# Turning the third and part of the fourth chunk of x2 while the second norm is found, in a trunk-layer kernel on one core

## The chip, the cores and the metric

The kernel runs on one core of one Trainium2 chip. The metric is the device time of one execution in microseconds (us); the median of several runs is given. The core's engines are TensorE (PE: matrix products and transposes, its weight loads are shown apart as PEld), VectorE (DVE), ScalarE (ACT), GpSimd (POOL) and SyncE (SP, which issues most DMAs).

## The reference

One transformer layer on 128 context tokens and 256 latent tokens, 384 in all, with model width 2048 and feed-forward width 5632, in float32. The part around the change, cut to what matters:

```python
x = x + g1 * token_mixing(...)                 # ends in a product with w_o
h2 = rms_norm(x, n2) * (1 + sc2) + sh2         # rms_norm(x, g) = x * rsqrt(mean(x*x) + eps) * g
a, g = split(h2 @ w_gate_up, 2)
x = x + g2 * ((silu(g) * a) @ w_down)
```

Context and latent tokens have different sc2, sh2, g1 and g2, so that every operation with them is done for two ranges of tokens.

## The kernel before

**Precision and weight units.** Every matrix product is done as three: both operands are split into a high and a low part (`split`, lines 133 to 135: the high part is a cast on ScalarE, L134, the low part a subtraction on VectorE, L135), and `mm3` (L138 to L140) adds high x high, high x low and low x high. Weights come in units of two blocks of 128 rows by 512 columns. `next_unit` splits the next loaded unit, steps the pieces of side work in `front` and `behind`, and returns the oldest split unit, whose matmuls are issued after it. Tags `wh` and `wl` have three buffers each, so a unit can be split when the third unit before it has been used up on TensorE; the units that are split and not yet used stand in the queue `ready`. In the last unit of the product with w_o nothing is split (`late`), so that ScalarE and VectorE are free for the norm; `split_unit` makes up for it after the first step of `normed`.

**Order.** The schedule is written out: each engine runs its instructions in the order in which the code issues them, and waits for others by semaphores. Side work is a Python generator in a `Paced`, which one tick of `next_unit` steps once.

**PSUM.** Eight banks: four buffers of tag `mm8` (`mm_tile`), three of tag `at8` (`at_tile`) and one for the modulation rows. `acc_tile` takes accumulators from a ring of four mm and then three at buffers. A new tile gets a buffer whose last user is done with it.

**Around the change.** The product with w_o runs over four chunks of 512 columns (`cc`), each with three accumulators (one for each 128 tokens) and eight units. After a chunk's last unit, `x2[cc]` = residual + gate x product (L1125, L1126), and the squares are summed for each token into `ssx[:, t, cc]` (L1128). In the next chunk's loop `transposed(cc - 1)` turns the chunk: for each 128 of its columns (`kt` counts them, 0 to 15), three TensorE transposes into one at buffer (L1096) and two ScalarE evictions with the norm's gain and modulation into `x2T` (L1098). So chunks 0, 1 and 2 are turned in the loops of chunks 1, 2 and 3.

After chunk 3 the norm is found: the reduction of `ssx` (L1132), then `inv_sqrt` (L152 to L159: mean and eps, square root on ScalarE, reciprocal and one Newton step). Its result per token, `r2`, is spread over the partitions by three transposes (L1140) and copied to `rB` (L1142). Then `normed` makes the operand h of the feed-forward part in steps of two `kt`: product with `rB` (L1148, VectorE), high parts with the shift (L1153, ScalarE), low parts (L1159, VectorE). Its first step runs before the feed-forward loop, each further one in a `next_unit`, so the step for the `kt` that a unit needs is issued one unit ahead. The steps k0 = 2, 4, 6, 8 also turn and evict one `kt` each of chunk 3 (12 to 15).

The first half of the feed-forward loop (`half` 1, part 0) has eight units, each 24 matmuls into four accumulators: unit u needs h of kt = u and u + 1. `facc` is None until the last of them, where the buffers for the rest are taken.

Of the kernel before, what the change touches and what calls it, by code (L numbers as in the profile page):

```python
# [13 lines left out]
F32 = mybir.dt.float32  # L14
F32R = mybir.dt.float32r
AF = mybir.ActivationFunctionType
ALU = mybir.AluOpType
AX = mybir.AxisListType

P = 128  # L20
D = 2048
KT = D // P
# [5 lines left out]
CTX = 128  # L28
LAT = 256
TOK = CTX + LAT  # L30
NT = TOK // P
# [64 lines left out]
def trunk_kernel(ctx: ExitStack, tc: tile.TileContext, io: dict):  # L96
    nc = tc.nc
# [26 lines left out]
    small = ctx.enter_context(tc.tile_pool(name="small", bufs=4))  # L124
# [19 lines left out]
        warm = small.tile([P, 1], F32, tag="warm", bufs=1, name=nm("warm"))  # L144
        nc.scalar.activation(out=warm, in_=ones[:, 0:1], func=AF.Sqrt)

    def inv_sqrt(out, ssq, n, shape):

        v = small.tile(shape, F32, tag="rs_v", name=nm("rsv"))
        s = small.tile(shape, F32, tag="rs_s", name=nm("rss"))  # L150
        t = small.tile(shape, F32, tag="rs_t", name=nm("rst"))
        nc.vector.tensor_scalar(v, ssq, 1.0 / n, EPS, op0=ALU.mult, op1=ALU.add)  # L152
        yield
        nc.scalar.activation(out=s, in_=v, func=AF.Sqrt)
        yield
        nc.vector.reciprocal(s, s)
        nc.vector.scalar_tensor_tensor(out=t, in0=s, scalar=-0.5, in1=s, op0=ALU.mult, op1=ALU.mult)
        nc.vector.tensor_mul(t, t, v)
        nc.vector.scalar_tensor_tensor(out=out, in0=t, scalar=1.5, in1=s, op0=ALU.add, op1=ALU.mult)  # L159
# [24 lines left out]
    front, behind = [], []  # L184
# [14 lines left out]
    def next_unit(late=False):  # L199

        for p in front:
            p.tick()
        if not late:
            split_unit()
        for p in front + behind:
            p.tick()
        loads.more()
        return ready.popleft()


    ident = consts.tile([P, P], F32, tag="ident", name="ident")
# [36 lines left out]
    msc = [consts.tile([P, KT, 2], F32, tag=f"msc{i}", name=f"msc{i}") for i in range(2)]  # L248
# [9 lines left out]
    with ExitStack() as ph:  # L258
# [7 lines left out]
        def at_tile():  # L266
            return pa.tile([P, CH], F32, tag="at", name=nm("at"))
# [3 lines left out]
        def acc_tile():  # L271

            return next(ring)()
# [146 lines left out]
        with ExitStack() as pha:  # L420
# [16 lines left out]
            for cc in range(4):  # L437
                t = c6([P, NT, CH], "xc")
# [14 lines left out]
            for j in range(2):  # L453
# [10 lines left out]
                out=csz[:, :, 0:2], in_=pt[:, 0:32].rearrange("p (c k) -> p k c", c=2), func=AF.Silu  # L464
# [5 lines left out]
            ssx = small.tile([P, NT, 4], F32, tag="ssx", bufs=1, name="ssx")  # L470
# [25 lines left out]
            ss1 = small.tile([P, NT], F32, tag="ss1", bufs=1, name="ss1")  # L496
            nc.vector.tensor_reduce(out=ss1, in_=ssx, axis=AX.X, op=ALU.add)
            r1 = small.tile([P, NT], F32, tag="r1", bufs=1, name="r1")
# [112 lines left out]
            for gi, (k0, n) in enumerate(GROUPS):  # L611
# [3 lines left out]
                for ci in ORDER:  # L615
# [3 lines left out]
                    for u in range(k0, k0 + n, 2):  # L619
# [3 lines left out]
                        for t in range(NT):  # L623
                            sl = slice(t * P, (t + 1) * P)
# [455 lines left out]
    def load_residual(cc):  # L1080
# [6 lines left out]
        rows_until(2)  # L1087
        yield from load_rows(xtp, 2, cc)

    def transposed(cc):  # L1090

        for k in range(4):
            kt = cc * 4 + k
            o = at_tile()
            for t in range(NT):
                nc.tensor.transpose(o[:, t * P : (t + 1) * P], x2[cc][:, t, k * P : (k + 1) * P], ident)  # L1096
            for cnd, sl in ((0, slice(0, CTX)), (1, slice(CTX, TOK))):
                nc.scalar.activation(  # L1098
                    out=x2T[cc][:, k, sl], in_=o[:, sl], func=AF.Copy, scale=msc[1][:, kt, cnd : cnd + 1]
                )  # L1100
            yield

    rows.rate = RATES[3]
# [1 line left out]
    for cc in range(4):  # L1105
        xin[cc] = xtp.tile([P, NT, CH], F32, tag="xin", bufs=2, name=nm("xin"))
        behind.append(Paced(load_residual(cc)))
        po = [acc_tile() for _ in range(NT)]
        for u in range(0, KT, 2):
            if cc == 3 and u == KT - 4:  # L1110
                rows.rate = 0
            if cc == 3 and u == 8:
                warm_sqrt()
            wH, wL = next_unit(late=cc == 3 and u == KT - 2)
            if u == 2 and cc:
                rows_until(4)
                behind.append(Paced(transposed(cc - 1)))
            for t in range(NT):
                sl = slice(t * P, (t + 1) * P)
                for kk in range(2):  # L1120
                    k = u + kk
                    mm3(po[t], mixH[k][:, sl], mixL[k][:, sl], wH[:, kk], wL[:, kk], k == 0, k == KT - 1)
                if u == KT - 2:
                    d = tmp.tile([P, CH], F32, tag="d", name=nm("d"))
                    nc.vector.tensor_mul(d, po[t], gb[cc][:, min(t, 1)])  # L1125
                    nc.vector.tensor_add(x2[cc][:, t], xin[cc][:, t], d)  # L1126
                    junk = tmp.tile([P, CH], F32, tag="junk", name=nm("junk"))
                    nc.scalar.activation(  # L1128
                        out=junk, in_=x2[cc][:, t], func=AF.Square, accum_out=ssx[:, t, cc : cc + 1]
                    )  # L1130
    ss2 = small.tile([P, NT], F32, tag="ss1", bufs=1, name="ss2")
    nc.vector.tensor_reduce(out=ss2, in_=ssx, axis=AX.X, op=ALU.add)  # L1132
    r2 = small.tile([P, NT], F32, tag="r1", bufs=1, name="r2")
    for _ in inv_sqrt(r2, ss2, D, [P, NT]):
        pass
    rows_until(3)
    last_chunk = transposed(3)
    o = mm_tile()
    for t in range(NT):
        nc.tensor.transpose(o[:, t * P : (t + 1) * P], r2[:, t : t + 1].to_broadcast([P, P]), ident)  # L1140
    rB = tmp.tile([P, TOK], F32, tag="rB", bufs=1, name="rB")
    nc.scalar.copy(rB, o[:, :TOK])  # L1142

    def normed():
        for k0 in range(0, KT, 2):
            for kt in (k0, k0 + 1):
                v = x2T[kt // 4][:, kt % 4]
                nc.vector.tensor_mul(v, v, rB)  # L1148
            for kt in (k0, k0 + 1):
                H, L = new_h(kt)  # L1150
                v = x2T[kt // 4][:, kt % 4]
                for cnd, sl in ((0, slice(0, CTX)), (1, slice(CTX, TOK))):
                    nc.scalar.activation(  # L1153
                        out=H[:, sl], in_=v[:, sl], func=AF.Identity, bias=msh[1][:, kt, cnd : cnd + 1]
                    )
            for kt in (k0, k0 + 1):
                v = x2T[kt // 4][:, kt % 4]
                for cnd, sl in ((0, slice(0, CTX)), (1, slice(CTX, TOK))):
                    nc.vector.scalar_tensor_tensor(  # L1159
                        out=hL[kt][:, sl], in0=v[:, sl], scalar=msh[1][:, kt, cnd : cnd + 1],  # L1160
                        in1=fr(hH[kt][:, sl]), op0=ALU.add, op1=ALU.subtract,
                    )
            if k0 in (2, 4, 6, 8):
                next(last_chunk)
            yield

    norm = Paced(normed())
# [6 lines left out]
    facc = None  # L1174
# [21 lines left out]
    for part, nf in enumerate(FF_PARTS):  # L1196
# [4 lines left out]
        cL = [None] * nf  # L1201
        for c4 in range(nf // 4):
            for half in (1, 0):
                po = [acc_tile() for _ in range(4)]
                for u in range(0, KT, 2):
                    wH, wL = next_unit()
                    if u == KT - 2 and facc is None:
                        norm.drain()
                        rows.rate = RATES[4]
                        pho.close()  # L1210
                        actp = phf.enter_context(tc.tile_pool(name="actp", bufs=1))
                        facc = [actp.tile([P, NT, CH], F32, tag=f"fa{i}", name=f"facc{i}") for i in range(4)]
                        ftmp = phf.enter_context(tc.tile_pool(name="tmpf", bufs=2))
                    for f in range(4):
                        s = slice(f * P, (f + 1) * P)
                        for kk in range(2):
                            k = u + kk
                            mm3(po[f][:, :TOK], wH[:, kk, s], wL[:, kk, s], hH[k], hL[k], k == 0, k == KT - 1)
                        if u < KT - 2:
                            continue  # L1220
                        if half:
                            if f == 0:
                                sg = ftmp.tile([P, 4, TOK], F32, tag="sg", name=nm("sg"))
                            nc.scalar.activation(out=sg[:, f], in_=po[f][:, :TOK], func=AF.Silu)
                        else:
                            i = c4 * 4 + f
                            nc.vector.tensor_mul(sg[:, f], sg[:, f], po[f][:, :TOK])
                            cH[i] = actp.tile([P, TOK], F32R, tag=f"cH{i}", name=nm("cH"))
                            cL[i] = actp.tile([P, TOK], F32R, tag=f"cL{i}", name=nm("cL"))
                            if nf == 4:  # L1230
                                split(cH[i], cL[i], sg[:, f])
            if nf > 4:
                behind.append(Paced(split_act(c4 * 4, sg, cH, cL), 2))
# [74 lines left out]
```

## Time and profile before

| | us |
|---|---|
| median of 3 runs (lowest, highest) | 2082.51 (2082.15, 2085.05) |
| the profiled execution | 2081.68 |
| its span, first to last instruction | 2079.9 |
| PE busy | 2045.1 (98%) |
| DVE busy | 1210.2 (58%) |
| ACT busy | 755.3 (36%) |
| POOL busy | 57.6 (3%) |
| mean granted TensorE clock | 0.998 of full speed |

The times of the prediction are us from the start of the span. The part that matters lies between the last loop of the product with w_o (its last matmul starts at 958.77) and the end of the first feed-forward half (about 1003.7). A busy TensorE isn't TensorE at its peak: matmuls overlap in the records, so a row's length is more than the distance to the next one's start. In a timeline, what stands in brackets is the idle time of the engine before the row, and what ended it.

### The profile page before, as it was taken

What the parts mean: (1) busy time and instruction counts of PE and PEld (TensorE: products, weight loads), DVE (VectorE), ACT (ScalarE), POOL (GpSimd) and SP (SyncE); (2) the same over time, 40 slices, a digit from 0 to 9 for tenths busy, and PEclk for the clock granted to TensorE, in tenths of its full rate; (3) what the DMA queues carried; (4) which work ended last, traced back from release to release, by engine and by line L of the source; (5) the groups of instructions that cost most, each with busy time, mean ns of one, the idle gap of its engine ahead of it and who ended that gap; (6) DMA issues with size and microseconds to landing.
All of it is one profiled execution on the core that took longest, in us unless ns stands there. A gap on an engine that the chain in (4) does not pass through costs nothing.

```text
span 2079.9 us, 27373 instructions
## 1 busy us (share of the span) xinstructions
PE 2045.1 (98%) x10963; PEld 1846.3 (89%) x10963; DVE 1210.2 (58%) x1418; ACT 755.3 (36%) x1146; POOL 57.6 (3%) x101
## 2 busy tenths in 40 slices
PE   6999999999999999998999999999999999999999
PEld 4668888999999999887998899899989998999897
DVE  4635899687885787665544454444454434333456
ACT  5323232456665443335333332223322232233222
POOL 3000000000001000001000000000000000000000
PEclk9999999999999999999999999999999999999999
DMA  9886878677775775753554555445454444444453
GB/s 343 287 321 212 299 246 306 208 215 226 221 218 156 262 247 174 263 189 116 162 159 145 155 160 155 145 146 157 158 153 140 122 126 128 124 130 122 132 162 121
DMA packets 219999, 390.45 MB, mean 188 GB/s; under 512 B 28080, under 2 KB 64960, under 8 KB 219872
## 3 DMA queue, kind: packets, MB, share of 16 engines
q1 hardware_dynamic: 212704, 382.13, 57.9%
q10 hardware_dynamic: 4672, 6.31, 0.8%
q8 instruction: 86, 1.41, 0.3%
q0 software_dynamic: 2496, 0.27, 0.1%
q14 instruction: 41, 0.34, 0.0%
HBM read 371.81 MB, written 20.51 MB: 189 GB/s over the span
## 4 chain that ended last, share of the span: by engine, by line
PE 93%; DVE 2%; DMA 2%; ACT 1%; issue 1%; SPq 1%; ACTq 0%; DVEq 0%
PE mm L138 19%; PE mm L139 19%; PE mm L140 19%; PE at L138 11%; PE at L139 11%; PE at L140 11%; DMA wm<-in_w_mod 1%; PE md L387 1%; DVE accr L311 1%; PE at L847 1%; PE at L915 1%; DVE wl L135 1%; DMA xc<-in_x_sample 0%; SPq L365 0%; PE md L321 0%
## 5 line engine op out<-in xcount | busy, mean ns | idle before, releaser
L135 DVE TENSOR_TENSOR wl<-wraw,wh 128x1024 fp32r<-128x1024 f32 (+1 forms) x464 | 559.5, 1206 | 711.1 <-ACT wh L134 710.1
L134 ACT CAST wh<-wraw 128x1024 fp32r<-128x1024 f32 (+1 forms) x464 | 480.1, 1036 | 1044.3 <-PE at L139 292.6
L138 PE MATMUL mm<-hH,wh 128*128 128x384 f32 x1216 | 410.7, 338 | 3.9 <-ACT gst L981 2.3
L140 PE MATMUL mm<-hH,wl 128*128 128x384 f32 x1216 | 406.8, 334 | 0.0
L139 PE MATMUL mm<-hL,wh 128*128 128x384 f32 x1216 | 406.4, 334 | 0.0
L311 DVE SCALAR_TENSOR_TENSOR accr<-wmr,csz,accr 128x1024 f32<-128x1024 f32 x240 | 304.8, 1278 | 0.0
L138 PE MATMUL at<-hH,wh 128*128 128x384 f32 x704 | 236.5, 336 | 1.4 <-ACT hH L1153 1.4
L138 PEld LDWEIGHTS mm<-hH,wh 128*128 128x128 f32 x1216 | 228.4, 188 | 9.5 <-ACT gst L981 3.5
L139 PE MATMUL at<-hL,wh 128*128 128x384 f32 x704 | 236.3, 336 | 0.0
L140 PE MATMUL at<-hH,wl 128*128 128x384 f32 x704 | 235.8, 335 | 0.0
L139 PEld LDWEIGHTS mm<-hL,wh 128*128 128x128 f32 x1216 | 228.4, 188 | 0.0
L140 PEld LDWEIGHTS mm<-hH,wl 128*128 128x128 f32 x1216 | 228.2, 188 | 0.0
L138 PE MATMUL mm<-wh,hH 128*128 128x512 f32 x431 | 172.6, 400 | 0.0
L139 PE MATMUL mm<-wl,hH 128*128 128x512 f32 x431 | 168.5, 391 | 1.7 <-DVE wl L135 1.7
L140 PE MATMUL mm<-wh,hL 128*128 128x512 f32 x431 | 168.1, 390 | 0.0
L138 PE MATMUL mm<-wh,cH 128*128 128x512 f32 x352 | 139.3, 396 | 0.0
L139 PE MATMUL mm<-wl,cH 128*128 128x512 f32 x352 | 139.2, 396 | 0.0
L140 PE MATMUL mm<-wh,cL 128*128 128x512 f32 x352 | 139.2, 396 | 0.0
L138 PEld LDWEIGHTS at<-hH,wh 128*128 128x128 f32 x704 | 132.7, 188 | 2.8 <-ACT hH L1153 1.8
L139 PEld LDWEIGHTS at<-hL,wh 128*128 128x128 f32 x704 | 132.7, 188 | 1.1 <-DVE hL L1159 0.7
L140 PEld LDWEIGHTS at<-hH,wl 128*128 128x128 f32 x704 | 132.6, 188 | 0.0
L138 PEld LDWEIGHTS mm<-wh,hH 128*128 128x128 f32 x431 | 81.0, 188 | 30.8 <-issue 9.8
(240 smaller groups left out, 2387.7 us busy)
## 6 DMA issues: line engine op xcount, KB each, us to landing
wraw<-in_w_gate_up SPq DMA_DIRECT2D x176, 512.0 KB, 3.7
wmr<-in_w_mod SPq DMA_DIRECT2D x128, 512.0 KB, 4.2
wraw<-in_w_down SPq DMA_DIRECT2D x88, 512.0 KB, 3.7
wm<-in_w_mod SPq DMA_DIRECT2D x64, 512.0 KB, 6.7
wraw<-in_w_gate SPq DMA_DIRECT2D x64, 512.0 KB, 5.1
wraw<-in_w_in SPq DMA_DIRECT2D x56, 512.0 KB, 5.9
wraw<-in_w_o SPq DMA_DIRECT2D x32, 512.0 KB, 5.2
wraw<-in_w_fnet_proj SPq DMA_DIRECT2D x16, 512.0 KB, 6.0
```

Source lines behind the costliest of these rows:

```text
L134: nc.scalar.copy(H, x)
L135: nc.vector.tensor_sub(L, x, fr(H))
L138: nc.tensor.matmul(out, aH, bH, start=start, stop=False)
L139: nc.tensor.matmul(out, aH, bL, start=False, stop=False)
L140: nc.tensor.matmul(out, aL, bH, start=False, stop=stop)
L311: nc.vector.scalar_tensor_tensor(out=acc[:, cnd], in0=wm, scalar=sc, in1=acc[:, cnd], op0=ALU.mult, op1=ALU.add)
L387: nc.tensor.matmul(pm[q : q + 32, :w], csz[:, k, :], wm[:, ty, kk + par, :], start=k < 2, stop=k >= KT - 2, tile_position=(0, q), skip_gro ...
L847: nc.tensor.matmul(po[j][:, cols], qx[rows[j], q], kx[rows[j], k], start=i == 0, stop=i == 2, tile_position=(j * HD, 0),)
L915: nc.tensor.transpose(o[:, i * P : (i + 1) * P], sc[:, j, c0 : c0 + P], ident)
```

## The change

Chunk 2 (kt 8 to 11) is no longer turned in the loop of chunk 3. Turning is cut in two functions: `turn` issues the transposes and keeps the tile in a queue `held`, `gained` issues the two evictions of the oldest tile there. After the norm, kt 8 and 9 are turned and evicted and kt 10 is turned; then come the transposes of `r2` and the copy to `rB`; then kt 11 and 12 are turned. Each step of `normed` evicts one held tile behind its own work and turns the next kt (13, 14, 15), until none is left. The reduction of `ssx` takes chunks 0 to 2 ahead of the last unit's matmuls, with the first operation of `inv_sqrt`; the sum of chunk 3 is added behind its squares by one operation. The accumulators of the first feed-forward half come from mm buffers alone and not from the ring.

```diff
-    def inv_sqrt(out, ssq, n, shape):
+    def inv_sqrt(out, ssq, n, shape, more=None):
...
         nc.vector.tensor_scalar(v, ssq, 1.0 / n, EPS, op0=ALU.mult, op1=ALU.add)
         yield
+        if more is not None:
+            nc.vector.scalar_tensor_tensor(out=v, in0=more, scalar=1.0 / n, in1=v, op0=ALU.mult, op1=ALU.add)
         nc.scalar.activation(out=s, in_=v, func=AF.Sqrt)
...
+    held = deque()
+
+    def turn(kt):
+        o = at_tile()
+        for t in range(NT):
+            nc.tensor.transpose(o[:, t * P : (t + 1) * P], x2[kt // 4][:, t, kt % 4 * P : (kt % 4 + 1) * P], ident)
+        held.append((kt, o))
+
+    def gained():
+
+        kt, o = held.popleft()
+        for cnd, sl in ((0, slice(0, CTX)), (1, slice(CTX, TOK))):
+            nc.scalar.activation(
+                out=x2T[kt // 4][:, kt % 4, sl], in_=o[:, sl], func=AF.Copy, scale=msc[1][:, kt, cnd : cnd + 1]
+            )
+
     def transposed(cc):
...
+        for kt in range(cc * 4, cc * 4 + 4):
+            turn(kt)
+            gained()
             yield
...
             wH, wL = next_unit(late=cc == 3 and u == KT - 2)
+            if cc == 3 and u == KT - 2:
+                ss2 = small.tile([P, NT], F32, tag="ss1", bufs=1, name="ss2")
+                nc.vector.tensor_reduce(out=ss2, in_=ssx[:, :, 0:3], axis=AX.X, op=ALU.add)
+                r2 = small.tile([P, NT], F32, tag="r1", bufs=1, name="r2")
+                norm = inv_sqrt(r2, ss2, D, [P, NT], ssx[:, :, 3])
+                next(norm)
             if u == 2 and cc:
                 rows_until(4)
-                behind.append(Paced(transposed(cc - 1)))
+                if cc < 3:
+                    behind.append(Paced(transposed(cc - 1)))
...
-    ss2 = small.tile([P, NT], F32, tag="ss1", bufs=1, name="ss2")
-    nc.vector.tensor_reduce(out=ss2, in_=ssx, axis=AX.X, op=ALU.add)
-    r2 = small.tile([P, NT], F32, tag="r1", bufs=1, name="r2")
-    for _ in inv_sqrt(r2, ss2, D, [P, NT]):
+
+    for _ in norm:
         pass
     rows_until(3)
-    last_chunk = transposed(3)
+    late = iter(range(8, KT))
+    for _ in range(2):
+        turn(next(late))
+        gained()
+    turn(next(late))
     o = mm_tile()
...
     nc.scalar.copy(rB, o[:, :TOK])
+    for _ in range(2):
+        turn(next(late))
...
-            if k0 in (2, 4, 6, 8):
-                next(last_chunk)
+            if held:
+                gained()
+            for kt in late:
+                turn(kt)
+                break
             yield
...
-                po = [acc_tile() for _ in range(4)]
+                po = [(acc_tile if facc else mm_tile)() for _ in range(4)]
```

More of the change, by code (lines that the diff above doesn't have):

```diff
@@ L1088, in load_residual @@
         yield from load_rows(xtp, 2, cc)
-    def transposed(cc):
[L1092 to L1100, printed above, removed]
+    held = deque()
[10 more added lines that the diff above has]
+            )
+    def transposed(cc):
+        for kt in range(cc * 4, cc * 4 + 4):
+            turn(kt)
+            gained()
             yield
```

## The prediction

> **What bounds the kernel now.** First the page's chain of work that ended last, then the same shares in a stretch of the last part of the kernel (columns: stretch in us, its length, busy us of PE, PEld, DVE, ACT and POOL with their counts, granted clock, DMA share, GB/s):
>
> ```profile
> PE 93%; DVE 2%; DMA 2%; ACT 1%; issue 1%; SPq 1%; ACTq 0%; DVEq 0%
> ```
>
> ```profile
> 1000.00:1100.00 100.00, 100.00 (x578) 99.88 (x577) 43.10 (x42) 31.81 (x38) 0.00 (x0) 1.00 0.53 164
> ```
>
> TensorE carries 93% of the chain, and from 1000 us on it is busy throughout. So a delay of its first feed-forward units reaches the end in full: nothing behind them has slack to give back. The change sits just ahead, where TensorE does wait. I call the eight weight units of the first feed-forward half A to H (k = 0,1 to 14,15); the stretches below run from each unit's first matmul to the next one's (PE's busy time, clock, DMA):
>
> ```profile
> 965.81:972.74 6.93, 6.52 (x27) 0.74 0.42 132
> 972.74:977.54 4.80, 4.74 (x30) 1.00 0.47 137
> 977.54:982.35 4.81, 4.74 (x30) 1.00 0.39 110
> 982.35:986.60 4.25, 4.25 (x28) 1.00 0.28 80
> 986.60:990.76 4.16, 4.16 (x26) 1.00 0.27 68
> 990.76:995.17 4.41, 4.41 (x25) 1.00 0.44 133
> 995.17:999.37 4.20, 4.20 (x26) 1.00 0.40 112
> 999.37:1003.70 4.33, 4.33 (x26) 1.00 0.46 132
> ```
>
> The fifth row is a unit at full speed, 4.16 us for 24 matmuls. Unit A takes 6.93 at a mean clock of 0.74. PE's timeline (start, length, engine, line, ...) shows the wait ahead of it:
>
> ```profile
> 959.09 0.24 PE L344 MATMUL md<-ident,colr 32*128 32x32 f32 x1
> 962.91 0.90 PE L1140 MATMUL mm<-ident,r 128*128 128x128 f32 x3 [3.58 <-DVE r L159]
> 963.61 0.85 PE L1096 MATMUL at<-ident,x 128*128 128x128 f32 x3
> 965.81 0.69 PE L138 MATMUL at<-hH,wh 128*128 128x384 f32 x1 [1.35 <-ACT hH L1153]
> ...
> 971.68 0.34 PE L140 MATMUL mm<-hH,wl 128*128 128x384 f32 x1
> 972.43 0.55 PE L1096 MATMUL at<-ident,x 128*128 128x128 f32 x3 [0.41 <-ACT x2T L1098]
> 972.74 0.42 PE L138 MATMUL at<-hH,wh 128*128 128x384 f32 x1
> ```
>
> TensorE idles 3.58 us for the second norm. Later one turn (three transposes, L1096) stands between units A and B and waits until ScalarE has evicted the tile turned before it. ScalarE's and VectorE's timelines give the reason and all durations I need:
>
> ```profile
> 961.86 0.20 ACT L154 ACTIVATE rss<-rsv 128x3 f32<-128x3 f32 x1 [0.43 <-DVE rsv L152]
> 963.85 0.48 ACT L1142 COPY rB<-mm 128x384 f32<-128x384 f32 x1 [1.79 <-PE mm L1140]
> 964.95 1.49 ACT L1153 ACTIVATE hH<-x2T,msh 128x128 fp32r<-128x128 f32 x4 [0.62 <-DVE x2T L1148]
> 966.35 1.98 ACT L134 CAST wh<-wraw 128x1024 fp32r<-128x1024 f32 x2
> 970.27 1.49 ACT L1153 ACTIVATE hH<-x2T,msh 128x128 fp32r<-128x128 f32 x4 [1.95 <-DVE x2T L1148]
> 971.67 0.71 ACT L1098 ACTIVATE x2T<-at,msc 128x128 f32<-128x128 f32 x2
> 972.28 1.04 ACT L134 CAST wh<-wraw 128x1024 fp32r<-128x1024 f32 x1
> 975.08 1.50 ACT L1153 ACTIVATE hH<-x2T,msh 128x128 fp32r<-128x128 f32 x4 [1.76 <-DVE x2T L1148]
> 976.48 0.71 ACT L1098 ACTIVATE x2T<-at,msc 128x128 f32<-128x128 f32 x2
> 977.09 1.05 ACT L134 CAST wh<-wraw 128x1024 fp32r<-128x1024 f32 x1
> ```
>
> ```profile
> 961.45 0.17 DVE L1132 TENSOR_REDUCE ss<-ssx 128x3 f32<-128x12 f32 x1 [0.85 <-ACT junk L1128]
> 961.65 0.17 DVE L152 TENSOR_SCALAR rsv<-ss 128x3 f32<-128x3 f32 x1
> ...
> 967.41 2.36 DVE L135 TENSOR_TENSOR wl<-wraw,wh 128x1024 fp32r<-128x1024 f32 x2 [0.45 <-ACT wh L134]
> 969.69 1.02 DVE L1148 TENSOR_TENSOR x2T<-x2T,rB 128x384 f32<-128x384 f32 x2
> 970.71 1.57 DVE L1159 SCALAR_TENSOR_TENSOR hL<-x2T,msh,hH 128x128 fp32r<-128x128 f32 x4
> 973.35 1.23 DVE L135 TENSOR_TENSOR wl<-wraw,wh 128x1024 fp32r<-128x1024 f32 x1 [1.06 <-ACT wh L134]
> 974.49 1.02 DVE L1148 TENSOR_TENSOR x2T<-x2T,rB 128x384 f32<-128x384 f32 x2
> ```
>
> The eviction runs 971.67 to 972.38 and the turn starts at 972.43: each engine keeps the order in which the code issues. There is also a closed loop without TensorE: weight cast 972.28, low part 973.35, product with rB 974.49, high parts of h 975.08, eviction 976.48, next cast 977.09. It lasts 4.81 us, and 0.61 of it (976.48 to 977.09) is the eviction; without one it is 4.20.
>
> **The change part by part.** I work on the clock of this profile and take the saving ahead of it off at the end.
>
> *Four turns fewer in chunk 3's accumulation.* The chain of waits prices one there:
>
> ```profile
> 942.10 0.33 PE at L1096 x3
> ```
>
> TensorE is the bound of that loop, so 4 x 0.33 = **1.3 us** go. Their eight evictions leave ScalarE, which had time there.
>
> *The sum in two steps.* L1132 and L152 now run ahead of the last unit's matmuls, on VectorE's idle time; behind the last square stands one small addition in place of two operations: 961.65 - 961.45 = **0.2 us** go. The addition itself is priced like its neighbours; if it cost nothing or twice as much, the sum moves by 0.2 either way.
>
> *Turns of 8 to 12 in the wait.* Three go ahead of the L1140 transposes, into 959.3 to 962.9: at 0.33 to 0.85 each 1.0 to 2.6 us, hidden. Two go behind them: 963.6 - 0.2 + 2 x 0.85 = 965.1, before unit A could start: hidden. If that cover were gone, they would cost 0.33 to 0.85 each. Evictions of 8 and 9 take 2 x 0.71 between the square root's end (962.06) and rB's copy (963.85): 1.4 in 1.79, hidden.
>
> *Turns of 13, 14 and 15.* This is the step that decides. The PSUM tag "at" has three buffers. Behind turn 12 the tiles 10, 11 and 12 hold all three. In each step of normed() the code now evicts one tile, behind that step's high parts on ScalarE, and then turns the next, which needs exactly that buffer. And the step is issued inside next_unit, ahead of the matmuls of the unit that is taken: turn 13 and turn 14 stand ahead of unit A on TensorE, turn 15 ahead of unit B. Before, two of these buffers belonged to accumulators, but a turn waited for the eviction of the step before; now it waits for that of its own.
>
> Turn 14 waits for the eviction of 11, which stands behind the casts for two units and behind the high parts for k = 2, 3. Before, that place in ScalarE's order was 971.67 (it evicted tile 12 there). The eviction of 10, now ahead of the two casts, adds 0.61; the norm's gain takes off 0.20. So it starts at 971.67 + 0.41 = 972.08, turn 14 at 972.43 + 0.41 = 972.84 and unit A at 972.74 + 0.41 = **973.15, not 965.81**. All matmuls of A and everything later are queued behind that wait.
>
> Unit A then takes 6.04 us (as before, 965.81 to 971.68 and 0.17), if the clock has fallen in the wait. Its last matmul starts at 979.02 and ends at 979.36, and only then is the buffer free for the cast of the fourth unit (tag wh has three). From that cast to the next turn it was 977.24 - 972.28 = 4.96 (976.48 and its 0.71, then 0.05); the turn takes 0.31 more. So turn 15 runs at 984.4 and **unit B starts at 984.7, not 972.74**. With 6.04 us again it ends at 990.7, and C follows at once, since its operands have long been ready.
>
> From D on the ScalarE/VectorE loop sets the pace. The second k of a unit needs its low part 974.49 - 972.28 + 1.02 + 1.57 = 4.80 behind the cast, and four matmul slots of 0.173 into the unit: start at cast + 4.11. The cast behind B is at 990.9, D at 995.0; evictions 13, 14 and 15 stretch the next three loops to 4.81: casts at 995.7, 1000.5 and 1005.3, units E, F and G at 999.8, 1004.6 and 1009.4. The next cast comes 4.20 later, at 1009.5, H at 1013.6, and with its 4.33 the half ends at 1017.9, against 1003.70. That is 14.2 later, less the 1.3 saved: **+12.9 us**.
>
> *mm_tile in the first half; the ring.* Four accumulators from the four mm buffers; the one that rB's transposes used is free after L1142, long before. The ring of accumulators is four places behind afterwards. No row shows that a place in it matters; with TensorE 100% busy there I take 0, bounds -0.5 and +0.5.
>
> *DMA.* No transfer is added or moved past a queue; SP's loads and POOL's rows come in the old order, some us later against TensorE.
>
> *The clock* is the open size. Its rows, one us or more each:
>
> ```profile
> 962.00:963.00 1.00, 0.09 (x1) 0.82 0.00 0
> 963.00:969.00 6.00, 4.65 (x15) 0.50 0.00 0
> 969.00:970.00 1.00, 1.00 (x6) 0.76 0.44 47
> ```
>
> An idle time of 3.58 us brought the clock to half by 962.64 (0.82 is 0.64 at 1 and 0.36 at 0.5), and it rose at 969.48. In the changed kernel TensorE idles about 5.3 us ahead of turn 14 (turn 13 ends at 964.95 - 0.2 + 1.40 + 0.71 + 0.05 + 0.55 = 967.5) and 5.0 ahead of turn 15. Both are longer, so I take the fall twice, at before's price 6.04 - 4.16 = 1.9 each. Bounds for each unit: 4.16 at full clock, and 7.7 if all 24 run at half (slots of 0.32), so +9.1 with neither and +16.2 with both wholly cold.
>
> [...]
>
> **The rivals.**
> 1. *The turns don't hold up the units* (a free buffer after all, or TensorE's order differs). Then only the loop counts: casts 972.7, 977.5, 982.3, 987.1, 991.9, 996.1, H at 1000.2 instead of 999.37: +0.8 for two more evictions in the loop, -1.3 ahead: -0.5, **2082.0**. Against it: at 972.43 a turn did wait for its buffer, and held B. It decides if a fourth buffer is free at turn 13. A gain over 4.2 us would need A warm as well (1.9) and the loop not binding.
> 2. *The clock stays up* in both waits: +9.1, **2091.6**. For it: a fall needs idle time at the right moment. Against it: 3.58 us sufficed.
> 3. *Both units wholly at half clock*: +16.2, **2098.7**. Against it: in A the clock rose after 3.67 us.
>
> **How the numbers follow.** The profiled execution took 2081.68, its span 2079.9; the median of the runs is 2082.51, 0.8 above. I put +12.9 on the median: **2095.4 us**. Chances: the stall with the clock falling about as before, in one or both units, 0.68; clock up 0.10; wholly cold 0.08; no stall 0.14, of which 0.10 is no change and 0.04 a gain over 0.2%. About 0.2% (4.2 us) is what a measurement of this kernel tells from no change. Cases 2 and 3 with 0.8 below and 0.3 above give the range **2090.8 to 2099.0**. Faster 0.04, same 0.10, slower 0.86.
>
> **What would show it.** Right: A starts about 14 us behind the last accumulation matmul (958.77 to 965.81, 7 us, before); the turn ahead of it waits for L1098's successor; a second idle time of about 5 us lies between A and B; low clock in both. The two small sums: no reduction behind the last square, and four turns fewer ahead of it. Wrong: A starts within 7 us, or turns 13 to 15 wait for no eviction.

## The result, and the profile after

| | before | after |
|---|---|---|
| median, us (6 runs each, the same chip) | 2082.88 | 2096.02 |
| lowest to highest, us | 2081.7 to 2085.05 | 2093.59 to 2099.32 |
| ratio (95% interval) | | 1.0061 (1.0051 to 1.0072) |
| the profiled execution and its span, us | 2081.68, 2079.9 | 2099.32, 2097.5 |

The changed kernel is 13.1 us slower; 12.9 were forecast. The profiled execution is the slowest of its six, and 4.8 us of its distance to before's profile arise ahead of the change: the first squares of chunk 0 start at 861.3 instead of 856.5, in a part that the diff doesn't touch. So the two are compared from a common point, the start of the last accumulation matmul of the product with w_o: 958.77 before, 962.17 after.

The stretches of the changed kernel, from just behind that accumulation to unit A and then from each unit's first matmul to the next one's (length, PE's busy time and count, granted clock, DMA share, GB/s):

```profile
962.62:976.45 13.83, 3.92 (x26) 0.69 0.22 68
976.45:988.37 11.92, 7.10 (x30) 0.79 0.18 52
988.37:994.15 5.78, 5.78 (x27) 0.71 0.02 6
994.15:998.31 4.16, 4.16 (x26) 1.00 0.15 17
998.31:1002.70 4.39, 4.39 (x26) 1.00 0.38 115
1002.70:1007.51 4.81, 4.73 (x25) 1.00 0.37 108
1007.51:1012.32 4.81, 4.73 (x26) 1.00 0.37 107
1012.32:1017.13 4.81, 4.73 (x26) 1.00 0.48 137
1017.13:1021.36 4.23, 4.23 (x26) 1.00 0.38 114
```

A starts 14.3 us behind the common point (7.0 before), the stretch of A is 11.9 long (6.9 before), units E to G take 4.81. The half ends at 1021.36, 59.19 behind the common point, against 44.93. From there to the end of the span it is 1076.1 us, and 1076.2 before: what was lost here is lost for good.

PE's timeline names the waits:

```profile
962.49 0.25 PE L347 MATMUL md<-ident,colr 32*128 32x32 f32 x1
962.67 1.22 PE L1098 MATMUL at<-ident,x 128*128 128x128 f32 x9
966.12 0.54 PE L1161 MATMUL mm<-ident,r 128*128 128x128 f32 x3 [2.23 <-DVE r L162]
966.49 0.82 PE L1098 MATMUL at<-ident,x 128*128 128x128 f32 x6
969.96 0.90 PE L1098 MATMUL at<-ident,x 128*128 128x128 f32 x3 [2.65 <-ACT x2T L1105]
975.89 0.90 PE L1098 MATMUL at<-ident,x 128*128 128x128 f32 x3 [5.04 <-ACT x2T L1105]
976.45 0.67 PE L138 MATMUL mm<-hH,wh 128*128 128x384 f32 x1
...
982.86 0.34 PE L140 MATMUL mm<-hH,wl 128*128 128x384 f32 x1
988.02 0.70 PE L1098 MATMUL at<-ident,x 128*128 128x128 f32 x3 [4.82 <-ACT x2T L1105]
988.37 0.67 PE L138 MATMUL mm<-hH,wh 128*128 128x384 f32 x1
```

The nine transposes at 962.67 are turns 8, 9 and 10 in the wait for the norm; it has shrunk to 2.23 us. The six at 966.49 are turns 11 and 12. So far the change does what it says. Then turn 13 waits 2.65 us, turn 14 waits 5.04 and turn 15 4.82, each for an eviction (L1105). ScalarE's timeline shows where these stand:

```profile
967.80 1.49 ACT L1176 ACTIVATE hH<-x2T,msh 128x128 fp32r<-128x128 f32 x4 [0.63 <-DVE x2T L1171]
969.20 0.71 ACT L1105 ACTIVATE x2T<-at,msc 128x128 f32<-128x128 f32 x2
969.80 1.98 ACT L134 CAST wh<-wraw 128x1024 fp32r<-128x1024 f32 x2
973.74 1.49 ACT L1176 ACTIVATE hH<-x2T,msh 128x128 fp32r<-128x128 f32 x4 [1.95 <-DVE x2T L1171]
975.13 0.71 ACT L1105 ACTIVATE x2T<-at,msc 128x128 f32<-128x128 f32 x2
983.05 1.04 ACT L134 CAST wh<-wraw 128x1024 fp32r<-128x1024 f32 x1 [7.21 <-PE mm L139]
985.86 1.49 ACT L1176 ACTIVATE hH<-x2T,msh 128x128 fp32r<-128x128 f32 x4 [1.76 <-DVE x2T L1171]
987.26 0.71 ACT L1105 ACTIVATE x2T<-at,msc 128x128 f32<-128x128 f32 x2
```

The eviction of 11 (975.13 to 975.84) lies behind two casts and the high parts for k = 2, 3, and turn 14 starts at 975.89. The cast at 983.05 had to wait 7.21 us for unit A to be used up; the eviction of 12 behind it ends at 987.97, and turn 15 follows at 988.02. TensorE waits for ScalarE, and ScalarE for TensorE.

### The profile page after: what moved, and what is told of

Same layout as the page of the kernel before. It is cut to its first block, busy times and chain, and to the rows that moved or that the text cites. A ratio compares the mean times of both kernels' runs of the same rounds, so it can differ in the third digit from the quotient of the medians.

```text
span 2097.5 us, 27374 instructions
## 1 busy us (share of the span) xinstructions
PE 2050.7 (98%) x10963; PEld 1850.2 (88%) x10963; DVE 1210.5 (58%) x1419; ACT 756.0 (36%) x1146; POOL 57.7 (3%) x101
## 4 chain that ended last, share of the span: by engine, by line
PE 52%; DVE 0%; ACT 0%; issue 0%; DVEq 0%; ACTq 0%
PE mm L139 10%; PE mm L138 10%; PE mm L140 10%; PE at L138 7%; PE at L140 7%; PE at L139 7%; ACT hH L1176 0%; DVE wl L135 0%; DVE d L1277 0%; DVE x L1278 0%; PE md L324 0%; ACT wh L134 0%; ACT x2T L1105 0%; DVE hL L1182 0%; DVE x2T L1171 0%; PE at L1098 0%
## 5 line engine op out<-in xcount | busy, mean ns | idle before, releaser
L138 PE MATMUL mm<-hH,wh 128*128 128x384 f32 x1408 | 477.9, 339 | 3.9 <-ACT gst L984 2.3
L139 PE MATMUL mm<-hL,wh 128*128 128x384 f32 x1408 | 473.7, 336 | 0.2
L140 PE MATMUL mm<-hH,wl 128*128 128x384 f32 x1408 | 473.3, 336 | 0.0
L138 PEld LDWEIGHTS mm<-hH,wh 128*128 128x128 f32 x1408 | 266.4, 189 | 11.1 <-ACT gst L984 3.5
L138 PE MATMUL at<-hH,wh 128*128 128x384 f32 x512 | 171.0, 334 | 0.0
L139 PE MATMUL at<-hL,wh 128*128 128x384 f32 x512 | 171.0, 334 | 0.0
L140 PE MATMUL at<-hH,wl 128*128 128x384 f32 x512 | 171.0, 334 | 0.0
L138 PE MATMUL at<-wh,cH 128*128 128x512 f32 x264 | 104.5, 396 | 0.0
L139 PE MATMUL at<-wl,cH 128*128 128x512 f32 x264 | 104.4, 396 | 0.0
L140 PE MATMUL at<-wh,cL 128*128 128x512 f32 x264 | 104.4, 396 | 0.0
```

The source lines that it names most:

```text
L138: nc.tensor.matmul(out, aH, bH, start=start, stop=False)
L139: nc.tensor.matmul(out, aH, bL, start=False, stop=False)
L140: nc.tensor.matmul(out, aL, bH, start=False, stop=stop)
```

## The experiments

Times are medians. The kernel before was run again beside each group of experiments, so its value differs a little, and a ratio always goes by the runs of its own group. Differences of one or two us are read from the timelines, one profile of each kernel: this table gives the start of units A, B, C and H and the end of the half in us behind the last accumulation matmul, worked out from each PE timeline by counting 24 matmuls a unit. A kernel with the turns of chunk 2 taken out of the accumulation has 1.37 us in hand there.

| kernel | A | B | C | H | end of half |
|---|---|---|---|---|---|
| before | 7.04 | 13.97 | 18.77 | 40.60 | 44.93 |
| after | 14.28 | 26.20 | 31.98 | 54.96 | 59.19 |
| two tiles held | 8.34 | 14.34 | 19.40 | 41.82 | 46.08 |
| a fourth buffer | 8.34 | 14.52 | 18.77 | 41.98 | 46.25 |
| busy waits | 14.04 | 23.61 | 27.86 | 50.83 | 55.09 |
| eviction first | 10.23 | 18.65 | 22.90 | 44.20 | 48.59 |
| two held, eviction first | 6.48 | 13.70 | 18.20 | 39.52 | 43.79 |
| the same, kept busy | 6.49 | 11.83 | 16.86 | 38.20 | 42.47 |
| before, mm buffers only | 7.05 | 13.21 | 17.73 | 40.63 | 44.95 |
| before, sum in two steps | 6.85 | 13.80 | 18.61 | 40.46 | 44.76 |

The theory: the loss is turns waiting for an eviction of their own step, and the low clock behind the waits. The rival: it is the two more evictions in the loop of ScalarE and VectorE (six instead of four).

**One tile less turned ahead.**

```diff
     nc.scalar.copy(rB, o[:, :TOK])
-    for _ in range(2):
+    for _ in range(1):
         turn(next(late))
```

> The changed kernel with one tile less turned ahead: behind rB only tile 11 is turned, so two tiles are held and the third at buffer is free in each step. Theory (the loss is the wait of turns 14 and 15 for an eviction of their own step): turn 13 now waits only for the eviction of 10, turn 14 for that of 11, one step earlier than in the changed kernel; unit A starts some 8.5 us behind the last accumulation matmul instead of 14.3, the 5 us of idle time between A and B go, and the time is about 2083 us, 13 under the changed kernel. Rival (the loss is the two more evictions in the loop of ScalarE and VectorE): they stay, so the time stays near 2095 us.

Measured: 2083.64 us against 2083.03 of the kernel before, ratio 1.0001 (0.9992 to 1.001). The whole loss is gone, with all six evictions still in the steps. A starts at 8.34. In its PE timeline, turns 13 and 14:

```profile
968.06 0.90 PE L1098 MATMUL at<-ident,x 128*128 128x128 f32 x3 [2.39 <-ACT x2T L1105]
974.37 0.49 PE L1098 MATMUL at<-ident,x 128*128 128x128 f32 x3
```

Turn 13 still waits, for the eviction of 10; turn 14 has no wait, and turn 15 waits 0.32 us. The rival falls as the cause of the 13 us: with all six evictions the half ends only 1.15 later than before (46.08 against 44.93).

**A fourth buffer for one tile.** Holding fewer tiles also changes what is turned when. This kernel leaves all that, and only gives tile 13 another bank:

```diff
     def turn(kt):
-        o = at_tile()
+        o = rows_psum["tile"]() if kt == 13 else at_tile()
```

> The changed kernel, in which tile 13 alone goes into the PSUM bank of the modulation rows (idle at that time), so that turns have four buffers and everything else, the place of the eviction and the tiles turned ahead among it, is as in the changed kernel. Theory (the wait for a buffer that the same step frees is the cause, and one more buffer ends it): turn 14 waits for the eviction of 10 and turn 15 for that of 11, each a step earlier; A about 8.5 us behind the last accumulation matmul instead of 14.3, no 5 us of idle time between A and B, time about 2083 us. Rival (turns ahead of rB or the ring of accumulators cost it): 2095 us still.

Measured: 2082.55 us against 2084.33, ratio 0.9989 (0.998 to 0.9998). Its PE timeline:

```profile
961.67 0.82 PE L1098 MATMUL at<-ident,x 128*128 128x128 f32 x6
962.33 0.65 PE L1098 MATMUL md<-ident,x 128*128 128x128 f32 x3
965.13 0.90 PE L1098 MATMUL at<-ident,x 128*128 128x128 f32 x3 [2.16 <-ACT x2T L1105]
971.62 0.49 PE L1098 MATMUL at<-ident,x 128*128 128x128 f32 x3
```

Tile 13 goes into md at once, turn 14 waits 2.16 us instead of 5.04, turn 15 not at all. One bank is the difference of 13 us (59.19 - 46.25 = 12.94 by the timeline), so the buffer is the cause and not the turns ahead of rB or the ring, which are both still there. By the timeline this kernel should equal the one before (46.25 - 44.93 - 1.37 = -0.05); whether it is a little faster, as the interval has it, stays open.

**Work for TensorE in the waits.**

```diff
             for kt in late:
+                idle = rows_psum["tile"]()
+                for _ in range({13: 16, 14: 38, 15: 36}[kt]):
+                    nc.tensor.transpose(idle[:, 0:P], x2[0][:, 0, 0:P], ident)
                 turn(kt)
```

> The changed kernel with 16, 38 and 36 additional transposes into an unused PSUM tile ahead of turns 13, 14 and 15, so that TensorE has work in the waits and its clock has no reason to fall; the waits themselves stay. Theory (of the 12.9 us, 9.1 are waits and 1.9 a unit are the low clock behind them): granted clock 1.0 in units A and B, A and B 4.2 us each, time about 2092 us, 4 under the changed kernel. Rival (the clock costs nothing of its own, since the loop of ScalarE and VectorE sets the pace anyway): time as the changed kernel, 2096 us, or more if the transposes outlast the waits.

Measured: 2091.34 us, ratio 1.0041 (1.0027 to 1.0054) to the kernel before; the changed kernel has 1.0061. The half ends 4.1 us earlier than in the changed kernel, where 3.8 was expected (1.9 a unit). Turns 14 and 15, and units A and B, each up to its last matmul:

```profile
971.62 0.55 PE L1098 MATMUL at<-ident,x 128*128 128x128 f32 x3 [0.70 <-ACT x2T L1105]
...
981.20 0.55 PE L1098 MATMUL at<-ident,x 128*128 128x128 f32 x3 [0.90 <-ACT x2T L1105]
```

```profile
971.93:976.20 4.27, 4.27 (x27) 1.00 0.10 38
981.50:985.75 4.25, 4.25 (x28) 1.00 0.02 8
```

The turns start where the evictions let them (that of 11 ends at 971.58, turn 14 starts at 971.62), so A starts only 0.24 earlier; the clock is 1.0 in A and B. By the timeline it is some 4 us of the loss, and the waits are the other 9. The two intervals, 1.0027 to 1.0054 and 1.0051 to 1.0072, overlap a little, so the 4 us rest on the timeline.

**The eviction at the head of the step**, with three tiles held:

```diff
         for k0 in range(0, KT, 2):
+            if held:
+                gained()
             for kt in (k0, k0 + 1):
...
-            if held:
-                gained()
             for kt in late:
```

> The changed kernel with the eviction at the head of each step of normed, ahead of that step's high parts on ScalarE, with three tiles held as in the changed kernel. Theory: turn 14 then waits for the casts of two units and not for the high parts behind them (A about 10.5 us behind the last accumulation matmul instead of 14.3), turn 15 for one cast behind A's end (2 us of idle time between A and B instead of 4.8, too short for the clock to fall), and the eviction lies in ScalarE's wait for VectorE, so that the loop is 4.2 us and not 4.81: time about 2085 us. Rival (only the number of buffers counts, not the place of the eviction): 2094 to 2096 us.

Measured: 2085.73 us, ratio 1.0011 (1.0002 to 1.002). A starts at 10.23. Turns 14 and 15:

```profile
967.00 0.90 PE L1098 MATMUL at<-ident,x 128*128 128x128 f32 x3 [3.08 <-ACT x2T L1105]
975.67 0.55 PE L1098 MATMUL at<-ident,x 128*128 128x128 f32 x3 [1.59 <-ACT x2T L1105]
```

3.08 and 1.59 us instead of 5.04 and 4.82: with the high parts no longer ahead of the eviction in ScalarE's order, the waits are 2 and 3.2 us shorter. Behind the 1.59 us B's matmuls start 0.17 us apart, as at full clock (0.32 apart at half clock, in A up to 972.1). The casts still stand ahead of it, and with all three buffers held the half still ends 3.66 later than before, of which the accumulation gives 1.37 back.

**Two tiles held and the eviction first**, the two edits together:

> Both: two tiles held, and the eviction at the head of each step. Theory: no turn waits for an eviction of its own step, and the loop is 4.2 us throughout; the turns of chunk 2 are out of the accumulation (1.4 us) and the evictions out of the loop (0.6 each): about 2079.5 us, 3 under the kernel before. Rival (the first feed-forward half is bound by TensorE, not by the loop, once no turn waits): 2082 us, as before.

Measured: 2080.84 us against 2083.03, ratio 0.9988 (0.998 to 0.9997). The half ends 1.14 earlier than before, and with the 1.37 in hand that is 2.5 us, inside the interval; 3 to 3.5 was expected. What is missing lies in A: 7.22 us from A to B, because A ran at half clock for 5.7 us of it, until 971.3. Three neighbouring stretches of 3.42 us and one that begins in the third and ends behind it, in this kernel (PE's busy time, clock):

```profile
961.02:964.44 3.42, 1.20 (x9) 1.00 0.00 0
964.44:967.86 3.42, 3.08 (x9) 0.50 0.00 0
967.86:971.28 3.42, 3.42 (x12) 0.50 0.46 135
971.00:972.00 1.00, 1.00 (x6) 0.87 1.11 361
```

**The same, with TensorE kept busy** ahead of A:

```diff
     o = mm_tile()
+    for _ in range(16):
+        nc.tensor.transpose(o[:, TOK:], x2[0][:, 0, 0:P], ident)
...
             for kt in late:
+                if kt == 13:
+                    idle = rows_psum["tile"]()
+                    for _ in range(6):
+                        nc.tensor.transpose(idle[:, 0:P], x2[0][:, 0, 0:P], ident)
                 turn(kt)
```

> Two tiles held and the eviction first, and besides 16 additional transposes into an unused part of a PSUM tile in the wait for the norm and 6 ahead of turn 13, so that TensorE's clock has less reason to fall ahead of unit A. Theory (A runs at half clock for most of its 24 matmuls, since the waits before it let the clock fall): A at clock 1.0 in 4.2 us; then the low parts for B are the next limit, so that B starts 1.8 us earlier and not 2.9, and H as much: about 2079 us, 1.8 under the version without them. Rival (the loop of ScalarE and VectorE takes up all of it): no gain, 2080.8 us.

Measured: 2079.15 us against 2084.33, ratio 0.9974 (0.9963 to 0.9984), the lowest of all versions; the interval overlaps that of the version without the extra transposes (0.998 to 0.9997), so what they add is read from the timeline. From the norm's wait through unit A:

```profile
959.00:962.00 3.00, 3.00 (x27) 1.00 0.01 3
962.00:965.00 3.00, 2.48 (x20) 1.00 0.00 0
965.00:968.00 3.00, 2.71 (x13) 1.00 0.00 0
968.00:971.00 3.00, 2.92 (x17) 1.00 0.61 170
```

The clock stays at 1.0. B starts 1.87 us earlier than without the extra transposes; 1.32 of it is left at the end of the half, where 1.8 was expected: B to C takes 5.03 instead of 4.50. By the timeline it gains 44.93 - 42.47 + 1.37 = 3.8 us on the kernel before, inside the measured interval.

**The mm buffers alone**, in the kernel before:

```diff
-                po = [acc_tile() for _ in range(4)]
+                po = [(acc_tile if facc else mm_tile)() for _ in range(4)]
```

> The kernel before, with the accumulators of the first feed-forward half taken from the mm buffers alone and nothing else changed, so that its turns 13 to 15 find a free buffer. Theory (with an eviction in it the loop of ScalarE and VectorE takes 4.81 us and sets the pace of the half, whatever the turns wait for): unit B starts 0.5 us earlier, but H still some 40.6 us behind the last accumulation matmul, time as before, 2083 us. Rival (TensorE's waits for the buffer set the pace): H 1.2 to 1.5 us earlier, 2081.5 us.

Measured: 2083.67 us against 2084.33, ratio 0.9993 (0.9984 to 1.0002). B starts 0.76 earlier, C 1.04, and H at 40.63 as before. The weight cast that was at 972.28 before and the three behind it start 13.53, 18.34, 23.16 and 27.97 us behind the last accumulation matmul, against 13.51, 18.32, 23.13 and 27.93 before: the loop of ScalarE and VectorE keeps its 4.81 us and takes all of it back.

**The sum in two steps alone**, in the kernel before (the hunks on inv_sqrt, ss2 and norm of the diff):

> The kernel before with the sum of squares in two steps and nothing else. Theory: 0.2 us less between the last square's sum and r2 (1.26 instead of 1.46), unit A 6.84 us behind the last accumulation matmul instead of 7.04, all later units as much earlier or unchanged; the time of one run cannot tell it from the kernel before, 2083 us. Rival (the early part of the sum delays the last gate product on VectorE): no gain there.

Measured: 2081.9 us, one run. A starts 0.19 earlier and the half ends 0.17 earlier. In VectorE's timeline one operation stands behind the last square, and r2 starts 1.04 us after it (962.70 - 961.45 = 1.25 before, with two).

```profile
961.87 0.16 DVE L155 SCALAR_TENSOR_TENSOR rsv<-ssx,rsv 128x3 f32<-128x3 f32 x1 [0.85 <-ACT junk L1136]
...
962.91 0.16 DVE L161 SCALAR_TENSOR_TENSOR r<-rst,rss 128x3 f32<-128x3 f32 x1
```

## Why the prediction was right

| step | forecast, us | measured, us |
|---|---|---|
| four turns out of the accumulation | -1.3 | -1.37 (squares of chunk 2 to those of chunk 3: 33.18 before, 31.81 after) |
| two-step sum | -0.2 | -0.20 (last square's sum to r2: 1.46 before, 1.26 after) |
| turns 8 to 12 and two evictions, hidden | 0 | 0 (the norm's wait is 2.23 instead of 3.58; rB's copy starts 0.56 earlier) |
| A behind the last accumulation matmul | 14.38 | 14.28 |
| A to B | 11.5 | 11.92 |
| loops with evictions 13 to 15 | 4.81 each | 4.81, 4.81, 4.81 |
| end of the half | 59.1 | 59.19 |
| ring of accumulators, rest of the kernel | 0 | 0 (1076.1 and 1076.2) |
| sum | +12.9 | +13.1 |

The mechanism was right: the eviction that frees a buffer and the turn that takes it stand in one step, in which the turn is ahead of a unit on TensorE and the eviction behind that step's work on ScalarE. The first rival turned on whether a buffer is free at turn 13. None was, and with one more buffer, or one held tile less, the loss goes.

Only sizes were off, and that they nearly cancel is luck. Turn 14 started 0.35 earlier than forecast, because the transposes of r2 ran at full clock behind turns 8 to 10 (0.54 us instead of 0.90), and took 0.25 longer at half clock. Two stretches show the clock under unit A:

```profile
976.00:981.00 5.00, 5.00 (x17) 0.50 0.13 50
981.00:982.00 1.00, 1.00 (x6) 0.77 0.00 0
```

A ran at half clock for 5.0 us (976.45 to about 981.5) and not for before's 3.67, so it took 6.58 instead of 6.04; B took 5.78, also instead of 6.04.

The reason given for the fall of the clock was too narrow. The prediction compared the idle time ahead of turn 14 with the 3.58 us of before. But the clock fell at 967.81, some 2 us before turn 13, at the end of a stretch that holds most of the norm's wait of 2.23 us, and it was low all through the long wait. Four stretches of the changed kernel:

```profile
964.40:967.81 3.41, 1.20 (x9) 1.00 0.00 0
971.22:974.64 3.42, 0.00 (x0) 0.50 0.39 97
981.46:984.88 3.42, 1.73 (x10) 1.00 0.00 0
984.88:988.29 3.41, 0.27 (x2) 1.00 0.53 145
```

The second stretch, without any work, lies in the wait ahead of turn 14; the wait ahead of turn 15 lies in the third and fourth, and the clock falls only behind the fourth. A runs partly at half clock with one held tile less and with the eviction first too (granted clock 0.50 from 966 to 971 and from 962 to 972, A from 968.61 and from 967.55), where the long wait of 5.04 us is gone or is 3.08 us. In the kernel with both, TensorE idles 2.23 us and a little later 0.55, and the clock falls all the same, at the end of a stretch with 1.20 busy us in 3.42.

## What to carry to other kernels

With all buffers of a tag held, taking the next tile is a wait for the oldest one's last reader (5.04 and 4.82 us here). See where that reader stands in its engine's order, and what stands behind the taker in its own: an eviction that is issued late and a turn that is issued early make one step's work a wait for the next unit. Keep one buffer free, and issue the release at the head of the step if you can: alone it took back most of the loss (2085.73 us instead of 2096.02), with the free buffer it made the kernel faster than before (ratio 0.9988). Filling the last buffer ahead of time bought nothing and cost 13 us.

Before work is moved into an idle time, count the waits that the move adds further on, and ask which loop sets the pace behind it: in the first feed-forward half TensorE's own waits could be removed without any gain, since the loop of ScalarE and VectorE took 4.81 us a unit with or without them.

## What the runs showed of the hardware

In these profiles the granted clock had the values 1 and 0.5, and it changed at distances that are multiples of 3.41 us. The times of its changes around the norm, worked out from stretches of 0.2 us with clocks of 1 and 0.5 as in the prediction, are 962.65 and 969.48 before; 967.81, 981.46, 988.29 and 991.70 after; 963.09 and 966.50 with busy waits; 961.86 and 972.10 with the eviction first. Within each of these profiles neighbouring changes lie 3.41, 6.83, 10.24 or 13.65 us apart, which is one, two, three or four times 3.41. Unit A started 3.67 us ahead of such a rise before (965.81) and 5.0 us ahead of one in the changed kernel (976.45), and ran at half clock for as long.

In stretches of 3.41 us that end at these changes, the clock fell at the end of stretches with 0.10 busy us (before), 1.48, 1.20 and 0.27 (the changed kernel), 1.24 (busy waits) and 1.20 (two tiles held, eviction first), and held behind one with 1.73 (the changed kernel, 981.46 to 984.88). The 1.48 belong to a wait of 1.93 us long ahead of the change, which both kernels have. Before, two stretches share it:

```profile
649.08 0.44 PE L138 MATMUL mm<-hH,wh 128*128 128x384 f32 x1 [1.93 <-ACT gst L981]
645.21:648.63 3.42, 1.94 (x14) 1.00 0.42 111
648.63:652.04 3.41, 2.96 (x17) 1.00 0.49 173
```

After, one stretch holds all of it:

```profile
652.34 0.44 PE L138 MATMUL mm<-hH,wh 128*128 128x384 f32 x1 [1.93 <-ACT gst L984]
650.37:653.78 3.41, 1.48 (x10) 1.00 0.65 211
653.78:657.20 3.42, 3.42 (x13) 0.50 0.50 178
```

The same wait left the clock at 1.0 in one profile and came ahead of 3.42 us at half clock in the other. So 1.93 us are neither always enough for a fall nor always too short for one, which is what the prediction's second rival says with the right moment. With two tiles held and the eviction first, waits of 2.23 and 0.55 us, one soon behind the other, came ahead of a fall.

At half clock, 3.08 busy us of 3.42 did not bring it back in the kernel with two tiles held and the eviction first (964.44 to 967.86), and wholly busy stretches did (966.06 to 969.48 before, 978.05 to 981.46 after); but so did one with 3.09, with the sum in two steps alone:

```profile
965.70:969.11 3.41, 3.09 (x9) 0.50 0.00 0
```

An estimate from these stretches: if the busy time of a stretch decides, the limit of the fall lies somewhere between 1.48 and 1.73 us. For the return the busy time of the records, in which the ends of matmuls are modelled, is too coarse: 3.08 and 3.09 can't be told apart.

Transposes into an unused tile kept the clock up or brought it back: with busy waits it rose at the end of a stretch with transposes alone, 963.09 to 966.50 (3.42 busy us of 3.42), and with 22 of them ahead of unit A it stayed at 1.0, which gained 1.3 us by the timeline.
